# Four padded tiles: another start address for the weight halves and the activations of a two-layer trunk on one core

## The chip, the cores and the metric

One core of one Trainium2 chip runs the whole program. The metric is the time of one execution on the device, in microseconds (us). The kernel before was run three times, and its time is the median of the three.

## The reference, cut to what matters

The kernel computes a two-layer decoder trunk over 256 positions and 2048 channels, in float32. Each layer normalises its input, multiplies it with a wide input matrix, mixes along the sequence (layer 0: dilated attention and gated linear attention; layer 1: a diagonal state-space model, "S5", and gated linear recurrence heads), gates the result and multiplies it with an output matrix:

```python
def ab_layer(h, w_in, gla_w_gate, gla_b_gate, gla_norm_g, w_out):
    z = h @ w_in
    qa, ka, va, qb, kb, vb, g_low, gate = jnp.split(z, AB_SPLIT, axis=-1)
    ya = dilated_attention(...)
    ...
    y = jnp.concatenate([ya, yb], axis=-1) * jax.nn.silu(gate)
    return y @ w_out

def cd_layer(h, w_in, ...):
    z = h @ w_in
    u, qd, fd, idd, gate = jnp.split(z, CD_SPLIT, axis=-1)
    yc = s5_mixer(u, ...)
    ...
    y = jnp.concatenate([yc, yd], axis=-1) * jax.nn.silu(gate)
    return y @ w_out

# reference: h = h + layer(rmsnorm(h, norm_g[l]), ...) for both layers, then a final rmsnorm
```

Nearly all of the arithmetic is in `h @ w_in`, `y @ w_out` and one product with `s5_w_glu` inside the S5 mixer.

## The kernel before, in words

**Three products for one.** Every float32 operand of the large products is split into a high and a low part of the type float32r: the weights into `wh` (L168, ScalarE, a rounding copy) and `wl` (L169, VectorE, the rest), the activations into `xh` and `xl` (or `yh` and `yl`). A product is then wh·xh + wh·xl + wl·xh, so three matmuls stand for one.

**The stream of weights.** `load_split` fetches one group of weights (four k-tiles of 128 rows by 512 columns, 1 MB) into `raw`, splits it in two halves of two k-tiles each, and gives the halves to the matmuls. `raw`, `wh` and `wl` have three buffers each, in the pool `stream`.

**Two orientations.** A matmul on TensorE holds a stationary operand of 128 columns, loaded before (LDWEIGHTS), while the columns of a moving operand stream past it.
- `gemm_fm` (matmul at L181, output with features on the partitions): stationary is a 128-column piece of `wh` or `wl`, moving are the 256 columns of one k-tile of the activations. Twelve matmuls for each k-tile.
- `gemm_tm` (matmul at L200, output with time on the partitions): stationary is half a k-tile of the activations (128 columns), moving are 512 columns of `wh` or `wl`. Six matmuls for each k-tile.
- The last 512 output columns are done in two halves of 256 by `mms` (L755), with the activations stationary and 256 columns moving. In the first half the moving operand lies in the weight halves of the pool `stream`. In the second half the split weights are put into `xh` and `xl`, which are free by then, and move from there.

The profile names the moving operand first: `pg<-xh,wl` is a matmul with xh moving and wl stationary.

**Which activations.** `xh`/`xl` feed every product of an input matrix in both layers. `yh`/`yl` are allocated twice: in the pool `yp` for layer 0's output projection (372 to 463 us of the profile, `gemm_fm`), and again in the pool `yp2` for the S5 product `wg` (736 to 764 us, `gemm_fm`) and layer 1's output projection (811 us to the end, `gemm_tm` and `mms`).

**What sets the order.** The order of instructions on each engine is fixed when the program is built. TensorE runs the matmuls of the large products one after the other, and the small matmuls of attention, gated attention and S5 are put between them. Weight loads are issued by SyncE's queue.

**Where the tiles lie.** Pools are laid out one behind the other in each partition's SBUF, each tile rounded up to 32 bytes. The order is `const`, `stream`, `mix`, `small`, and then a stack: first `att`, with `prep` and later `yp` above it; after `att` and `yp` are closed, `gz`, with `s5` and later `yp2` above it. Sizes of `raw` (8192 bytes), `wh`, `wl` (4096 bytes each) and `xh`, `xl`, `yh`, `yl` (16384 bytes each, 1024 for a k-tile) are multiples of 512 bytes, as is the step of 128 columns (512 bytes) from one stationary piece to the next. So every buffer of one kind, and every piece of it that a matmul begins with, has the same start modulo 512 bytes. In the program before these starts are:

| tile (pool) | first byte in a partition | modulo 512 |
|---|---|---|
| xh, xl (const) | 33792, 50176 | 0 |
| ones (const) | 86816 | 288 |
| raw, wh, wl (stream) | 99936, 124512, 136800 | 96 |
| gq, gk, gv and others (mix) | 155232, 159328, 167520 | 96 |
| pT (att) | 191296 | 320 |
| yh, yl (yp) | 192832, 209216 | 320 |
| gz0, gz1 (gz) | 181056, 185152 | 320 |
| yh, yl (yp2) | 189248, 205632 | 320 |

Of the kernel before, what the change touches and what calls it, by code (L numbers as in the profile page):

```python
# [12 lines left out]
F32 = mybir.dt.float32  # L13
# [7 lines left out]
S = 256  # L21
# [36 lines left out]
def trunk(ctx: ExitStack, tc: tile.TileContext, I, out):  # L58
# [3 lines left out]
    const = ctx.enter_context(tc.tile_pool(name="const", bufs=1))  # L62
# [9 lines left out]
    def urgent():  # L72
        return tc.high_priority(offset=HI)
# [6 lines left out]
    oT = const.tile([128, KT, S], F32, name="oT")  # L80
    cst = const.tile([128, NCST], F32, name="cst")
    msk = const.tile([128, len(LV), 32], I32, name="msk")
    ones = const.tile([128, 128], F32, name="ones")
    sqa = const.tile([128, 4, S], F32, name="sqa")
    ident = cst[:, C_ID:C_ID + 128]

# [3 lines left out]
    def pm_tile(name="pm"):  # L90
        return pm.tile([128, 512], F32, name=name, tag="pm")
# [21 lines left out]
    def finish_norm(tag):  # L113
        V.tensor_add(sqa[:, 0:2], sqa[:, 0:2], sqa[:, 2:4])
        V.tensor_add(sqa[:, 0], sqa[:, 0], sqa[:, 1])
        ps = pm_tile()
        for t in range(2):
            T.matmul(ps[:, t:t + 1], sqa[:, 0, t * 128:(t + 1) * 128], ones[:, 0:1], start=True, stop=True)
        ms = small.tile([128, 2], F32, name="nms")
        V.tensor_scalar(ms, ps[:, 0:2], 1.0 / D, EPS, op0=OP.mult, op1=OP.add)  # L120
        rc = const.tile([128, 2], F32, name=tag + "c")
        rsqrt(rc, ms, 2, "nr")
        pb = pm_tile()
        for t in range(2):
            dg = small.tile([128, 128], F32, name="dg")
            V.tensor_scalar(dg, ident, rc[:, t:t + 1], None, op0=OP.mult)
            T.matmul(pb[:, t * 128:(t + 1) * 128], ones, dg, start=True, stop=True)
        rb = const.tile([128, S], F32, name=tag + "b")
        A.activation(rb, pb[:, 0:S], AF.Copy)
        return rc, rb  # L130
# [62 lines left out]
    def gemm_tm(src, groups, ah, al, mid=None, order=None):  # L193
        ps = pg.tile([128, 2, 512], F32, name="pg")
        last = groups * 4 - 1
        for i, kt, wh, wl in _iter(src, groups, mid, order):
            for n, (w, a) in enumerate(((wh, ah), (wh, al), (wl, ah))):
                for t in range(2):
                    ts_ = slice(t * 128, (t + 1) * 128)
                    state["mm"] = T.matmul(ps[:, t], a[:, kt, ts_], w, start=(i == 0 and n == 0),  # L200
                                           stop=(i == last and n == 2), skip_group_check=True)
        return ps
# [8 lines left out]
    def gla_tiles():  # L211
        return (mix.tile([128, 4, S], F32, name="gf"), mix.tile([128, 4, S], F32, name="gq"),
                mix.tile([128, 4, S], F32, name="gk"))

    att = ExitStack()
    ap_ = att.enter_context(tc.tile_pool(name="att", bufs=1))
# [23 lines left out]
    f, q, k = gla_tiles()  # L240
# [167 lines left out]
    def attention(h, q, k, v, vc):  # L408
        pr = ap_.tile([128, 2, S], F32, name="pr", bufs=1)
        mx = small.tile([128, 2], F32, name="amx")  # L410
        den = small.tile([128, 2], F32, name="aden")
        ps = pm_tile().rearrange("p (t j) -> p t j", t=2)
        for t in range(2):
            n = 128 * (t + 1)
            T.matmul(ps[:, t, 0:n], q[:, t * 128:(t + 1) * 128], k[:, 0:n], start=True, stop=True)  # L415
        for t in range(2):
            n = 128 * (t + 1)
            V.scalar_tensor_tensor(pr[:, t, 0:n], ps[:, t, 0:n], rsc[:, t:t + 1], bias[:, t, 0:n],
                                   op0=OP.mult, op1=OP.add)
            V.tensor_reduce(mx[:, t:t + 1], pr[:, t, 0:n], axis=mybir.AxisListType.X, op=OP.max)  # L420
        V.tensor_scalar(mx, mx, -1.0, None, op0=OP.mult)
        for t in range(2):
            n = 128 * (t + 1)
            A.activation(pr[:, t, 0:n], pr[:, t, 0:n], AF.Exp, bias=mx[:, t:t + 1], accum_out=den[:, t:t + 1])
        V.reciprocal(den, den)
        for t in range(2):
            n = 128 * (t + 1)
            V.tensor_scalar(pr[:, t, 0:n], pr[:, t, 0:n], den[:, t:t + 1], None, op0=OP.mult)
        pt = pm_tile()
        for n, (t, j) in enumerate(((0, 0), (1, 0), (1, 1))):  # L430
            T.transpose(pt[:, n * 128:(n + 1) * 128], pr[:, t, j * 128:(j + 1) * 128], ident)
        pT = ap_.tile([128, 384], F32, name="pT", bufs=1)
        A.activation(pT, pt[:, 0:384], AF.Copy)
        po = pm_tile()
        T.matmul(po[:, 0:256], v[:, 0, vc:vc + 128], pT[:, 0:256], start=True, stop=False)
        T.matmul(po[:, 128:256], v[:, 1, vc:vc + 128], pT[:, 256:384], start=False, stop=True)
        A.activation(oT[:, h], po[:, 0:256], AF.Copy)
# [14 lines left out]
    def heads(qk, h):  # L452
        for n in range(2):
            attention(h + n, qk[:, n], qk[:, 2 + n], v, (h + n) * 128)
# [34 lines left out]
    def gate_tm(src, rc, zs):  # L489
        ps = gemm_tm(src, 4, xh, xl)  # L490
        z = zs.rearrange("p a s -> p (a s)").rearrange("p (t d) -> p t d", t=2)
        with urgent():
            for t in range(2):
                A.activation(z[:, t], ps[:, t], AF.Silu, scale=rc[:, t:t + 1])
        return z
# [34 lines left out]
    with urgent():  # L530
        rc1, rb1 = finish_norm("r1")
# [3 lines left out]
    w1 = I["w1"]  # L535
    gz = ctx.enter_context(tc.tile_pool(name="gz", bufs=1))
# [124 lines left out]
    for half in range(2):  # L661
        f, q, k = gla_tiles()
# [8 lines left out]
        v = mix.tile([128, 2, 512], F32, name="gv")  # L671
        evac_tm(v, 0, gemm_tm(w1[4 + 3 * half], 4, xh, xl), rc1)
        gla(f, q, k, v, 128, 512 * half)
    zs2 = [gate_tm(w1[10 + n], rc1, gz.tile([128, 4, S], F32, name=f"gz{n}")) for n in range(2)]
    while fillq:
        hook()
    sp.close()
# [440 lines left out]
def build(arrays):  # L1118
    nc = bacc.Bacc("TRN2", target_bir_lowering=False, num_devices=1)
    I = {k: nc.dram_tensor("in_" + k + "_dram", v.shape, mybir.dt.from_np(v.dtype), kind="ExternalInput").ap()  # L1120
         for k, v in arrays.items()}
    out = nc.dram_tensor("out_0_dram", (2, 128, D), F32, kind="ExternalOutput").ap()
    with tile.TileContext(nc, schedule_with_timeline_sim=True) as tc:
        trunk(tc, I, out)
    if not nc.is_finalized():
        nc.finalize()
    return nc
# [8 lines left out]
```

## Time and profile before

| | us |
|---|---|
| median of 3 runs (912.89, 913.5, 915.94) | 913.5 |
| the profiled execution, its own time | 916.01 |
| its span, first to last instruction | 914.1 |
| TensorE busy in the span (98%) | 898.6 |
| VectorE busy (70%) | 637.1 |
| ScalarE busy (52%) | 472.1 |

The mean granted clock of TensorE is 0.993. The program moves 180.40 MB by DMA, 197 GB/s on average. Matmuls are pipelined: the busy time of one matmul overlaps that of the next, so the time that a stream of matmuls costs is read from the distance between the starts of successive ones, the pitch. The timeline merges consecutive matmuls with the same operands into a row (x4 is four of them) and gives the start of the first.

### The profile page before, as it was taken

What the parts mean: (1) busy time and instruction counts of PE and PEld (TensorE: products, weight loads), DVE (VectorE), ACT (ScalarE), POOL (GpSimd) and SP (SyncE); (2) the same over time, 40 slices, a digit from 0 to 9 for tenths busy, and PEclk for the clock granted to TensorE, in tenths of its full rate; (3) what the DMA queues carried; (4) which work ended last, traced back from release to release, by engine and by line L of the source; (5) the groups of instructions that cost most, each with busy time, mean ns of one, the idle gap of its engine ahead of it and who ended that gap; (6) DMA issues with size and microseconds to landing.
All of it is one profiled execution on the core that took longest, in us unless ns stands there. A gap on an engine that the chain in (4) does not pass through costs nothing.

```text
span 914.1 us, 18689 instructions
## 1 busy us (share of the span) xinstructions
PE 898.6 (98%) x7728; PEld 820.6 (90%) x7728; DVE 637.1 (70%) x1197; ACT 472.1 (52%) x715; POOL 54.4 (6%) x106
## 2 busy tenths in 40 slices
PE   9999899999999999999999999999999999999995
PEld 9987699978998899999999998799877799988885
DVE  7986874889859868755575585776987756555562
ACT  7554445665654765644443334445455465444451
POOL 0001100112101101000000001000100000000000
PEclk9999899999999999999999999999999999999998
DMA  9726643686746645555576665664643554555532
GB/s 319 304 102 204 225 177 142 195 271 219 261 186 218 219 179 184 191 185 185 185 276 197 242 235 192 222 207 142 223 169 116 200 204 157 187 177 182 185 138 92
DMA packets 40388, 180.40 MB, mean 197 GB/s; under 512 B 12720, under 2 KB 14256, under 8 KB 22768
## 3 DMA queue, kind: packets, MB, share of 16 engines
q1 hardware_dynamic: 29440, 154.99, 48.1%
q0 software_dynamic: 7984, 22.69, 7.5%
q10 hardware_dynamic: 2880, 1.54, 0.6%
q8 instruction: 60, 0.98, 0.4%
q14 instruction: 24, 0.20, 0.1%
HBM read 166.48 MB, written 12.71 MB: 196 GB/s over the span
## 4 chain that ended last, share of the span: by engine, by line
PE 94%; DMA 2%; DVE 1%; issue 1%; ACT 0%; POOL 0%; SPq 0%; POOLq 0%; DVEq 0%
PE pg L181 53%; PE pg L200 30%; PE pg L755 2%; PE pm L287 1%; PE pm L339 1%; DMA E<-ed 1%; PE pm L621 1%; PE pm L625 1%; PE pm L583 1%; PE pm L308 1%; PE pm L415 1%; DMA ed<-et 1%; PE pm L1024 1%; PE pm L504 0%; PE pm L711 0%
## 5 line engine op out<-in xcount | busy, mean ns | idle before, releaser
L168 ACT ACTIVATE wh<-raw 128x1024 fp32r<-128x1024 f32 (+2 forms) x276 | 287.7, 1046 | 350.9 <-PE pg L181 206.3
L169 DVE TENSOR_TENSOR wl<-raw,wh 128x1024 fp32r<-128x1024 f32 (+2 forms) x276 | 332.6, 1207 | 179.4 <-ACT wh L168 174.5
L181 PE MATMUL pg<-xh,wl 128*128 128x256 f32 x1024 | 167.3, 283 | 0.0
L181 PE MATMUL pg<-xh,wh 128*128 128x256 f32 x1024 | 166.2, 283 | 0.5 <-ACT wh L168 0.5
L181 PE MATMUL pg<-xl,wh 128*128 128x256 f32 x1024 | 165.8, 282 | 0.0
L181 PEld LDWEIGHTS pg<-xh,wh 128*128 128x128 f32 x1024 | 140.1, 189 | 1.9 <-ACT wh L168 1.2
L181 PEld LDWEIGHTS pg<-xh,wl 128*128 128x128 f32 x1024 | 140.7, 189 | 1.0 <-DVE wl L169 0.3
L181 PEld LDWEIGHTS pg<-xl,wh 128*128 128x128 f32 x1024 | 140.6, 189 | 0.6 <-issue 0.3
L200 PE MATMUL pg<-wl,xh 128*128 128x512 f32 x320 | 103.2, 403 | 3.0 <-DVE wl L169 3.0
L200 PE MATMUL pg<-wh,xl 128*128 128x512 f32 x320 | 102.8, 401 | 0.0
L200 PE MATMUL pg<-wh,xh 128*128 128x512 f32 x320 | 102.5, 401 | 0.0
L200 PEld LDWEIGHTS pg<-wl,xh 128*128 128x128 f32 x320 | 59.8, 190 | 18.2 <-DVE wl L169 4.0
L200 PEld LDWEIGHTS pg<-wh,xl 128*128 128x128 f32 x320 | 60.4, 190 | 14.5
L200 PEld LDWEIGHTS pg<-wh,xh 128*128 128x128 f32 x320 | 60.1, 190 | 14.0
L181 PE MATMUL pg<-yh,wh 128*128 128x256 f32 x320 | 51.3, 281 | 0.0
L181 PE MATMUL pg<-yh,wl 128*128 128x256 f32 x320 | 50.8, 281 | 0.0
L181 PE MATMUL pg<-yl,wh 128*128 128x256 f32 x320 | 50.8, 281 | 0.0
L181 PEld LDWEIGHTS pg<-yh,wh 128*128 128x128 f32 x320 | 43.6, 188 | 0.0
L181 PEld LDWEIGHTS pg<-yl,wh 128*128 128x128 f32 x320 | 43.5, 188 | 0.0
L181 PEld LDWEIGHTS pg<-yh,wl 128*128 128x128 f32 x320 | 43.4, 188 | 0.0
L964 POOL DMA_DIRECT2D tabs<-pc x44 | 23.8, 547 | 167.0 <-DVE x L974 42.6
L200 PE MATMUL pg<-wh,yh 128*128 128x512 f32 x96 | 30.4, 398 | 0.0
(350 smaller groups left out, 1008.9 us busy)
## 6 DMA issues: line engine op xcount, KB each, us to landing
raw<-in_w_dram SPq DMA_DIRECT2D x100, 1024.0 KB, 5.0
raw<-in_wo_dram SPq DMA_DIRECT2D x28, 1024.0 KB, 4.8
tb<-tabs POOLq DMA_DIRECT2D x8, 768.0 KB, 6.3
tabs<-pc POOLq DMA_DIRECT2D x20, 256.0 KB, 5.5
raw<-in_wg_dram SPq DMA_DIRECT2D x4, 1024.0 KB, 4.8
raw<-in_wo1l_dram SPq DMA_DIRECT2D x4, 1024.0 KB, 4.8
raw<-in_w_dram SPq DMA_DIRECT2D x6, 512.0 KB, 7.6
tabs<-pc POOLq DMA_DIRECT2D x24, 128.0 KB, 4.3
```

The lines of the kernel that those rows point to most:

```text
L168: state["wh"] = A.activation(w, r, AF.Copy)
L169: V.tensor_sub(l, r, w)
L181: state["mm"] = T.matmul(ps[:, c], w[:, cs], a[:, kt], start=(i == 0 and n == 0 and c % 2 == 0), stop=(i == last and n == 2), skip_group_c ...
L200: state["mm"] = T.matmul(ps[:, t], a[:, kt, ts_], w, start=(i == 0 and n == 0), stop=(i == last and n == 2), skip_group_check=True)
L287: T.matmul(ps[32 * b:32 * b + 32, t, hd], k[:, hd, r], Q[:, hd, r], start=True, stop=True)
L308: T.matmul(ps[j0:j0 + h, hd, j0 + h:j0 + 2 * h], k[:, hd, b:b + h], Qp[:, hd, b + h:b + 2 * h], start=True, stop=True)
L339: T.matmul(ps[:, (hd - h0) * dv:(hd - h0 + 1) * dv], AT[:, hd, t + j], v[:, j, hd * dv:(hd + 1) * dv], start=(j == 0), stop=(j == t))
L415: T.matmul(ps[:, t, 0:n], q[:, t * 128:(t + 1) * 128], k[:, 0:n], start=True, stop=True)
L583: T.matmul(pv[g * 64:g * 64 + 64, w, pr], t["W"][w][us, 4 * h + pr], X[us, g, 4 * h + pr], start=True, stop=True)
L621: T.matmul(py[g * 64:g * 64 + 64, pr], w[:, pr], X[:, g, pr], start=(pr == 0), stop=False, skip_group_check=True)
L755: T.matmul(ps[:, t, 0:256], a_[:, kt, ts_], w_, start=(kt == 0 and n == 0), stop=(kt == KT - 1 and n == 2), skip_group_check=True)
L964: nc.gpsimd.dma_start(tabs[qt, dst, n], t[src].rearrange("p a b -> p (a b)"))
```

## The change

Four tile declarations get columns behind their data that nothing reads or writes. No instruction is added, removed or given another shape; only start addresses change.

```diff
-    ones = const.tile([128, 128], F32, name="ones")
+    ones = const.tile([128, 128 + 56], F32, name="ones")[:, 0:128]
...
-        pT = ap_.tile([128, 384], F32, name="pT", bufs=1)
+        pT = ap_.tile([128, 384 + 8], F32, name="pT", bufs=1)[:, 0:384]
...
-    zs2 = [gate_tm(w1[10 + n], rc1, gz.tile([128, 4, S], F32, name=f"gz{n}")) for n in range(2)]
+    zs2 = [gate_tm(w1[10 + n], rc1, gz.tile([128, 4 * S + 24 * n], F32, name=f"gz{n}")[:, 0:4 * S]
+                   .rearrange("p (a s) -> p a s", a=4)) for n in range(2)]
```

The 56 columns behind `ones` (224 bytes) move everything laid out after it by 224 bytes. The 8 columns behind `pT` (32 bytes) move `prep` and `yp` by 32 more. Behind `gz0` stand 24·0 = 0 columns, behind `gz1` 24 (96 bytes), which move `s5` and `yp2` by 96 more. Modulo 512 bytes this gives:

| tile | before | after |
|---|---|---|
| xh, xl | 0 | 0 |
| raw, wh, wl, and the pool mix | 96 | 320 |
| yh, yl of layer 0 (yp) | 320 | 320 + 256 = 64 |
| yh, yl of layer 1 (yp2) | 320 | 320 + 320 = 128 |

## The prediction

> **What bounds the kernel now.** I read the page first: engine shares, the chain that ended last, the costliest groups. Then the waits of TensorE, and then the timeline, where the change has to show.
>
> ```profile
> PE 898.6 (98%) x7728; PEld 820.6 (90%) x7728; DVE 637.1 (70%) x1197; ACT 472.1 (52%) x715; POOL 54.4 (6%) x106
> PE 94%; DMA 2%; DVE 1%; issue 1%; ACT 0%; POOL 0%; SPq 0%; POOLq 0%; DVEq 0%
> L168 ACT ACTIVATE wh<-raw 128x1024 fp32r<-128x1024 f32 (+2 forms) x276 | 287.7, 1046 | 350.9 <-PE pg L181 206.3
> L181 PE MATMUL pg<-xh,wl 128*128 128x256 f32 x1024 | 167.3, 283 | 0.0
> L200 PE MATMUL pg<-wl,xh 128*128 128x512 f32 x320 | 103.2, 403 | 3.0 <-DVE wl L169 3.0
> L181 PE MATMUL pg<-yh,wh 128*128 128x256 f32 x320 | 51.3, 281 | 0.0
> L200 PE MATMUL pg<-wh,yh 128*128 128x512 f32 x96 | 30.4, 398 | 0.0
> L755 PE MATMUL pg<-wh,yh 128*128 128x256 f32 x32 | 9.0, 282 | 0.0
> PE pg L200 <- DVE wl L169: 3.0, 2, 2.8
> PE pg L181 <- ACT wh L168: 0.5, 1, 0.5
> ```
>
> TensorE is busy for 98% of the span and holds 94% of the chain. It waits for data 3.0 + 0.5 us, while ScalarE's rounding copy stands idle 206.3 us behind the L181 matmuls because its buffers are still in use. So the time is the number of matmuls times their pitch. The groups give the numbers, each with three products: feature-major with xh/xl 3 x 1024 = 3072, with yh/yl 3 x 320 = 960, time-major 3 x (320 + 96) = 1248, and at L755 32 a group, 96 in each half. A mean of 283 ns is no price, since matmuls overlap; the pitch is. The timeline gives it from the first and the last row of an undisturbed stretch:
>
> ```profile
> 488.01 0.63 PE L181 MATMUL pg<-xh,wh 128*128 128x256 f32 x4
> ...
> 507.72 0.51 PE L181 MATMUL pg<-xh,wh 128*128 128x256 f32 x3
> ...
> 777.80 0.63 PE L181 MATMUL pg<-xl,wh 128*128 128x256 f32 x4
> ...
> 797.73 0.52 PE L181 MATMUL pg<-xl,wh 128*128 128x256 f32 x3
> ...
> 375.48 0.63 PE L181 MATMUL pg<-yl,wh 128*128 128x256 f32 x4
> ...
> 399.61 0.64 PE L181 MATMUL pg<-yl,wh 128*128 128x256 f32 x4
> ...
> 174.03 0.63 PE L200 MATMUL pg<-wh,xh 128*128 128x512 f32 x2
> ...
> 193.62 0.63 PE L200 MATMUL pg<-wh,xh 128*128 128x512 f32 x2
> ...
> 811.88 0.63 PE L200 MATMUL pg<-wl,yh 128*128 128x512 f32 x2
> ...
> 832.88 0.40 PE L200 MATMUL pg<-wl,yh 128*128 128x512 f32 x1
> ...
> 881.11 0.28 PE L755 MATMUL pg<-wh,yh 128*128 128x256 f32 x1
> ...
> 891.61 0.28 PE L755 MATMUL pg<-wh,yh 128*128 128x256 f32 x1
> ...
> 893.33 0.28 PE L755 MATMUL pg<-xh,yh 128*128 128x256 f32 x1
> ...
> 896.73 0.28 PE L755 MATMUL pg<-xh,yh 128*128 128x256 f32 x1
> ```
>
> The pairs are 168, 168, 204, 84, 90, 90 and 30 matmuls apart (whole k-tiles of 12 or 6, or whole rounds of three products). With the starts modulo 512 bytes from the table above, written stationary/moving:
>
> - feature-major, xh: 96/0, two rates: 19.71 us / 168 = 117.3 ns and 19.93 / 168 = 118.6
> - feature-major, yh: 96/320: 24.13 / 204 = 118.3
> - time-major, 512 columns, xh: 0/96: 19.59 / 84 = 233.2; yh: 320/96: 21.00 / 90 = 233.3
> - L755, first half, 256 columns: 320/96: 10.50 / 90 = 116.7
> - L755, second half, 256 columns: 320/0: 3.40 / 30 = **113.3**
>
> The last two are the key. They have the same shape, the same kind of operands and the same stationary tile; only the moving operand starts at 0 instead of 96, and the pitch falls by 3.3 ns. The first line has the same moving start 0 and the same width as the last, but stationary 96 instead of 320, and is 4.0 to 5.3 ns slower. So, as far as these rows go, the pitch depends on start addresses, and 96 is a bad start on either side. I read 96 as bad because it isn't a multiple of 64, as 0, 64, 128 and 320 are; the rows fit that, but show no other odd start, so it is a guess.
>
> **The change part by part.** No instruction, DMA, wait or buffer is added or removed, and the order in each queue stays. What moves is the residue pairs:
>
> 1. Feature-major with xh/xl, 3072 matmuls, 96/0 becomes **320/0**: the pair of the 113.3 row. Their clean pitches run from 117.3 to 118.6; I take 118.0, near the middle. 3072 x (118.0 - 113.3) = 14.4 us. Bounds: gain 14.4; loss, if the new pair falls to the worst pitch at 256 columns that the trace has, 120 ns (rows below), 3072 x 2.0 = 6.1 us.
> 2. Feature-major with yh/yl, 960, 96/320 becomes 320/64 (768 in the output projection) and 320/128 (192 in `wg`). No row has a moving start of 64 or 128. Bounds: 113.3 and 120, so -4.8 to +1.6 us. I take -4.8, because 320 as stationary and starts that are multiples of 64 are what the 113.3 row has.
> 3. Time-major, 1248, 0/96 and 320/96 become 0/320 and 320/128. The stationary start made no difference (233.2 against 233.3), and 233.3 is twice the 116.7 of 256 columns at the same moving 96. If moving away from 96 saves per column what it saves at L755, 512 columns go to 2 x 113.3 = 226.7: -6.7 ns x 1248 = -8.3 us. If what is left at 113.3 is partly a price per matmul, more falls away. Other bound: 2 x 120, +8.3 us. I take -8.3.
> 4. L755: first half 320/96 becomes 128/320, 96 x -3.3 ns = -0.3 us. Second half 320/0 becomes 128/0: it has the best row now, so nothing to -0.3 and up to 96 x 6.7 = +0.6 us; I take nothing.
> 5. The casts at L168 and L169, the loads and the small matmuls: source and destination of the casts move together, by 224 bytes. I cost them at nothing: ScalarE waits on TensorE here, and VectorE has the cover of the next rows. If each of the 276 casts on VectorE were a tenth longer (0.12 of 1.2 us), the busiest stages would come to its limit.
>
> ```profile
> L169 DVE TENSOR_TENSOR wl<-raw,wh 128x1024 fp32r<-128x1024 f32 (+2 forms) x276 | 332.6, 1207 | 179.4 <-ACT wh L168 174.5
> 0.00:30.00 30.00, 28.46 (x202) 27.72 (x203) 24.77 (x91) 22.59 (x37) 1.76 (x7) 1.00 0.94 342
> 172.00:220.00 48.00, 48.00 (x238) 38.51 (x238) 40.38 (x89) 28.80 (x55) 7.63 (x14) 1.00 0.76 247
> 76.72 5.07 DMA ed<-et
> 82.07 10.14 DMA E<-ed
> 94.80 1.15 DVE wl L169
> ```
>
> The columns of the two windows are length, then busy time of PE, PEld, DVE, ACT, POOL, then clock, DMA share, GB/s. Two places don't give their gain back in full. In the first 30 us the weights come at 342 GB/s with the DMA engines busy for 0.94, so TensorE can't run ahead of the loads. From 76.72 to 95.95 us the chain runs through S5's two transfers (5.07 and 10.14 us) and VectorE. These 49 us are 5% of the span: 5% of 27.8 is 1.5 us. VectorE, busy for 40.38 of 48.00 us, would be at 40.38 / 46.6 = 87% after a stage 3% shorter: no bound, but it may delay a cast once or twice, 0.5 us as an estimate from the 3.0 us that it costs now. I take off 2 us.
>
> Sum: 14.4 + 4.8 + 8.3 + 0.3 - 2.0 = 25.8 us against the profiled execution's 916.0: **890**. That execution is 2.5 us above the median. The two rates of 96/0 can make such a difference (3072 x 1.3 ns = 4.0 us between all slow and all fast). The other pairs show one rate, so I expect the new kernel at one level and don't take the 2.5 us off again.
>
> [...]
>
> **The rivals.**
>
> *Only the pair that the trace has gets faster.* The new pairs at 64, 128 and 0/320 keep their pitches and step 1 alone stands: 916.0 - 14.4 + 1 = 903; with step 2 or step 3 beside it 894 to 898. For it: a rule from two good starts is thin. Against: 96/0 and 96/320 both lie at 117 to 118.6, so nothing shows 320 as moving start to be worse than 0.
>
> *The change doesn't do what it says in the feature-major stream.* The 113.3 row differs from L181 in more than addresses: L181 sends successive matmuls to four parts of two PSUM banks and moves the same columns four times, L755 stays in one part and changes the moving columns. If that makes the 4 to 5 ns, steps 1 and 2 bring nothing, and only time-major gains: 916.0 - 8.3 = 908, or, without it, 914, the old time.
>
> *Slower: the new pairs clash.* If the two reads of one matmul disturb each other by their distance, not by a bad start, a new distance can be worse. A row for it is a small product with stationary `glhl` (320 and steps of 128 bytes on) and xh or xl moving at 0:
>
> ```profile
> 49.39 0.28 PE L372 MATMUL pm<-xh,glhl 128*32 128x256 f32 x1
> ...
> 52.87 0.28 PE L373 MATMUL pm<-xl,glhl 128*16 128x256 f32 x1
> ```
>
> 3.48 us / 29 = 120 ns, slower than any other stream of 256 columns, though every start is a multiple of 64. Its stationary operand is only 32 or 16 columns wide, so I don't take it for the rule. If feature-major fell to 120 ns: 6.1 + 1.6 = +7.7 us, 924. It decides from the point where the feature-major pitch passes 118.0 with time-major unchanged.
>
> **How the numbers follow.** All steps as costed: 0.48, 884 to 895 by its own bounds. Only part of them (893 to 904): 0.22. Nothing in feature-major: 0.16 (0.07 near 908, 0.09 unchanged). Slower, 924: 0.14. A measurement here can tell 0.3% from no change, 2.7 us: 910.8 to 916.2. That gives faster 0.48 + 0.22 + 0.07 = 0.77, same 0.09, slower 0.14. The range must reach to the unchanged time to leave out no more than 2 in 10: 882 to 914; 882 allows for time-major some 6 ns better than 226.7, less the losses.
>
> **What would show it.** In the profile after: feature-major pitch with xh at 113.3 in the clean stretches (step 1), with yh in the output projection at 113.3 (step 2), time-major at 226.7 (step 3), each at one rate. TensorE still near 98% busy, its waits for `wl` and `wh` under 6 us in sum (step 5). L755's second half unchanged (step 4). The prediction is wrong if the feature-major pitch with 320/0 isn't that of the L755 row, if a moving start of 64, 128 or 320 costs what 96 costs, or if VectorE's casts become the chain.

## The result, and the profile after

The kernel after takes 898.8 us (median of four, 898.14 to 899.84) against 913.5 us: ratio 0.9835, 95% interval 0.9815 to 0.9855. The profiled execution took 898.85 us, its span is 897.0 us. The prediction was 890 in a range of 882 to 914: the time lies inside the range, 9 us over the sum.

From the page of the kernel after, the engine shares and the chain by engine, then two waits of TensorE, as before:

```profile
PE 880.9 (98%) x7728; PEld 806.7 (90%) x7728; DVE 636.2 (71%) x1197; ACT 472.5 (53%) x715; POOL 54.4 (6%) x106
PE 88%; DVE 4%; DMA 2%; ACT 2%; issue 2%; SPq 0%; POOL 0%; POOLq 0%; DVEq 0%
PE pg L181 <- ACT wh L168: 2.3, 3, 1.1
PE pg L200 <- DVE wl L169: 0.5, 2, 0.3
```

TensorE's busy time fell by 17.7 us, the span by 17.1; VectorE and ScalarE are as they were. TensorE's part of the chain fell from 94% to 88%, and the rest runs through casts, loads and issue, but its waits stay small (2.3 + 0.5 us for `wh` and `wl`). So it is still mainly the pitch. The timeline of TensorE in the kernel after, first and last row of a stretch for each pair (L755 is now L756):

```profile
485.37 0.62 PE L181 MATMUL pg<-xh,wh 128*128 128x256 f32 x4
...
504.41 0.62 PE L181 MATMUL pg<-xh,wh 128*128 128x256 f32 x4
...
31.55 0.64 PE L181 MATMUL pg<-xh,wh 128*128 128x256 f32 x4
...
38.62 0.64 PE L181 MATMUL pg<-xh,wh 128*128 128x256 f32 x4
...
435.59 0.64 PE L181 MATMUL pg<-yh,wh 128*128 128x256 f32 x4
...
451.43 0.64 PE L181 MATMUL pg<-yh,wh 128*128 128x256 f32 x4
...
735.72 0.63 PE L181 MATMUL pg<-yh,wh 128*128 128x256 f32 x4
...
746.55 0.63 PE L181 MATMUL pg<-yh,wl 128*128 128x256 f32 x4
...
165.45 0.62 PE L200 MATMUL pg<-wh,xl 128*128 128x512 f32 x2
...
184.68 0.62 PE L200 MATMUL pg<-wh,xl 128*128 128x512 f32 x2
...
816.94 0.63 PE L200 MATMUL pg<-wh,yl 128*128 128x512 f32 x2
...
837.47 0.63 PE L200 MATMUL pg<-wh,yh 128*128 128x512 f32 x2
...
863.13 0.28 PE L756 MATMUL pg<-wh,yl 128*128 128x256 f32 x1
...
873.38 0.28 PE L756 MATMUL pg<-wh,yl 128*128 128x256 f32 x1
```

The counts between are 168, 60, 132, 92, 84, 88 and 87 matmuls. As stationary/moving modulo 512 bytes:

| matmuls | pair before | ns before | pair after | ns after | foretold |
|---|---|---|---|---|---|
| feature-major xh, 3072 | 96/0 | 117.3 or 118.6 | 320/0 | 113.3, in places 117.8; mean 114.0 | 113.3 |
| feature-major yh, layer 0, 768 | 96/320 | 118.3 | 320/64 | 120.0 | 113.3 |
| feature-major yh, `wg`, 192 | 96/320 | 118.4 | 320/128 | 117.7 | 113.3 |
| time-major xh, 960 | 0/96 | 233.3 | 0/320 | 228.9 to 229.2 | 226.7 |
| time-major yh, 288 | 320/96 | 233.3 | 128/320 | 233.3 | 226.7 |
| L756 first half, 96 | 320/96 | 116.7 | 128/320 | 117.8 | 113.3 |

### The profile page after: what moved, and what is told of

Its sections match the earlier page's. It is cut to its first block, busy times and chain, and to the rows that moved or that the text cites. A ratio compares the mean times of both kernels' runs of the same rounds, so it can differ in the third digit from the quotient of the medians.

```text
span 897.0 us, 18689 instructions
## 1 busy us (share of the span) xinstructions
PE 880.9 (98%) x7728; PEld 806.7 (90%) x7728; DVE 636.2 (71%) x1197; ACT 472.5 (53%) x715; POOL 54.4 (6%) x106
## 4 chain that ended last, share of the span: by engine, by line
PE 88%; DVE 4%; DMA 2%; ACT 2%; issue 2%; SPq 0%; POOL 0%; POOLq 0%; DVEq 0%
PE pg L181 51%; PE pg L200 26%; PE pg L756 2%; PE pm L287 1%; PE pm L339 1%; PE pm L621 1%; DMA E<-ed 1%; PE pm L625 1%; DVE wl L169 1%; DMA raw<-in_w_dram 1%; PE pm L583 1%; PE pm L308 1%; PE pm L415 1%; PE pm L1025 1%; ACT wh L168 1%
## 5 line engine op out<-in xcount | busy, mean ns | idle before, releaser
L181 PE MATMUL pg<-xh,wh 128*128 128x256 f32 x1024 | 161.8, 279 | 2.3 <-ACT wh L168 2.3
L181 PE MATMUL pg<-xh,wl 128*128 128x256 f32 x1024 | 163.1, 280 | 0.1
L181 PE MATMUL pg<-xl,wh 128*128 128x256 f32 x1024 | 161.1, 278 | 0.0
L181 PEld LDWEIGHTS pg<-xh,wh 128*128 128x128 f32 x1024 | 136.6, 188 | 4.0 <-ACT wh L168 3.4
L181 PEld LDWEIGHTS pg<-xh,wl 128*128 128x128 f32 x1024 | 136.9, 188 | 1.3 <-DVE wl L169 0.5
L181 PEld LDWEIGHTS pg<-xl,wh 128*128 128x128 f32 x1024 | 136.7, 188 | 0.6 <-issue 0.3
L200 PE MATMUL pg<-wl,xh 128*128 128x512 f32 x320 | 101.0, 396 | 0.7 <-DVE wl L169 0.5
L200 PE MATMUL pg<-wh,xl 128*128 128x512 f32 x320 | 100.7, 394 | 0.0
L200 PE MATMUL pg<-wh,xh 128*128 128x512 f32 x320 | 100.3, 394 | 0.0
L200 PEld LDWEIGHTS pg<-wl,xh 128*128 128x128 f32 x320 | 59.1, 188 | 14.2 <-DVE wl L169 1.6
L200 PEld LDWEIGHTS pg<-wh,xl 128*128 128x128 f32 x320 | 59.8, 188 | 12.9
L200 PEld LDWEIGHTS pg<-wh,xh 128*128 128x128 f32 x320 | 59.3, 188 | 12.8
L181 PE MATMUL pg<-yh,wh 128*128 128x256 f32 x320 | 51.8, 283 | 0.0
L181 PE MATMUL pg<-yh,wl 128*128 128x256 f32 x320 | 51.3, 282 | 0.0
L181 PE MATMUL pg<-yl,wh 128*128 128x256 f32 x320 | 51.3, 282 | 0.0
L181 PEld LDWEIGHTS pg<-yh,wh 128*128 128x128 f32 x320 | 44.1, 191 | 0.0
L181 PEld LDWEIGHTS pg<-yl,wh 128*128 128x128 f32 x320 | 44.0, 191 | 0.0
L181 PEld LDWEIGHTS pg<-yh,wl 128*128 128x128 f32 x320 | 44.0, 191 | 0.0
L200 PE MATMUL pg<-wh,yh 128*128 128x512 f32 x96 | 30.4, 397 | 0.0
```

The costliest lines, as they stand in the source:

```text
L181: state["mm"] = T.matmul(ps[:, c], w[:, cs], a[:, kt], start=(i == 0 and n == 0 and c % 2 == 0), stop=(i == last and n == 2), skip_group_c ...
```

## The experiments

Theory 1, the prediction's: each start counts by itself, multiples of 64 are good. It was in trouble at once, since 320/64 and 128/320 are no better than before. Theory 2: the distance from the stationary to the moving start decides. Theory 3: the trunk's other work sets the pitch.

**1. and 2. All pairs, alone.** A program without the trunk: 16 stationary by 16 moving starts, 32 bytes apart, 48 matmuls of 256 columns a pair (bench256), or 28 of 512 (bench512).

```python
p = ps.tile([128, 512], F32, name="s" + chr(97 + i) + "m" + chr(97 + j), tag="p")
for r in range(REPS):
    c, k = r % PIECES, (r // PIECES) % 2
    T.matmul(p[:, 0:N], sta[:, 8*i + 128*c:8*i + 128*c + 128], mov[:, 8*j + N*k:8*j + N*k + N], ...)
```

> This program leaves out the trunk: it runs 256 streams of 48 matmuls of 256 columns, one stream for each pair of a stationary start (letter after s: a = 0, b = 32, ... p = 480 modulo 512 bytes) and a moving start (letter after m), the four stationary pieces in turn as in the feature-major product, and nothing else beside them. Theory 1, own start: what counts is whether each of the two starts is a multiple of 64. Then the 64 pairs with two such starts run at 113.3 ns and the others at 116.7 to 118.7. Theory 2, distance: the pitch depends on moving minus stationary start modulo 512 alone, one value on each diagonal: 113.3 at 192, 120 at 256, about 118 at 224 and 320, 117.3 or 118.7 at 416, 116.7 at 288. Theory 3, neither: 320/0, 320/64 and 320/128 don't come out at the 113.3, 120.0 and 117.8 of the kernel after, so that the trunk's other work sets the pitch; then the table is flat or has another order.

> This program leaves out the trunk: as the one with 256 columns, but 28 matmuls of 512 columns a stream with two stationary pieces in turn, as in the time-major product. Own start: all pairs with a moving start that is a multiple of 64 run alike, faster than 233.3 ns. Distance: one value on each diagonal, 229.1 ns where moving minus stationary is 320, 233.3 at 96, 192 and 288. If the trunk's other work sets the pitch, the 0/320 stream doesn't come out near 229.1.

From the timelines, stationary start 32 (`sb`), moving 32, 64, 96 and 288, 320, 352, first 256 columns, then 512. Columns are start and length in us:

```profile
107.82 5.92 PE L82 MATMUL sbmb<-mov,sta 128*128 128x256 f32 x48
113.57 5.82 PE L82 MATMUL sbmc<-mov,sta 128*128 128x256 f32 x48
119.23 5.82 PE L82 MATMUL sbmd<-mov,sta 128*128 128x256 f32 x48
...
153.36 5.92 PE L82 MATMUL sbmj<-mov,sta 128*128 128x256 f32 x48
159.11 5.82 PE L82 MATMUL sbmk<-mov,sta 128*128 128x256 f32 x48
164.77 5.82 PE L82 MATMUL sbml<-mov,sta 128*128 128x256 f32 x48
```

```profile
120.52 6.53 PE L82 MATMUL sbmb<-mov,sta 128*128 128x512 f32 x28
126.89 6.70 PE L82 MATMUL sbmc<-mov,sta 128*128 128x512 f32 x28
...
172.53 6.53 PE L82 MATMUL sbmj<-mov,sta 128*128 128x512 f32 x28
178.90 6.70 PE L82 MATMUL sbmk<-mov,sta 128*128 128x512 f32 x28
```

A stream and the one 256 bytes further have the same length, and at one distance all 16 stationary starts agree, the first stream of all (48 matmuls in 8.34 us, 174 ns each) and the two distances with two pitches aside. Means of the later part of each stream, good to some 0.3 ns:

| moving minus stationary, modulo 256 bytes | 0 | 32 | 64 | 96 | 128 | 160 | 192 | 224 |
|---|---|---|---|---|---|---|---|---|
| 256 columns, ns | 120.0 | 117.8 | 117.8 | 120.1 | 118.5 | 118.6 or 117.3 | 117.8 or 113.3 | 118.3 |
| 512 columns, ns | 226.7 | 233.3 | 229.1 | 233.2 | 233.1 | 234.3 | 233.3 | 233.3 |

Theory 2 is right among starts that are multiples of 32, with a period of 256, not 512. Every pitch of the trunk, before and after, stands in this table but L755's first half before (116.7 at distance 32, where the table has 117.8; the pair 0/32 stands at 116.7 in the programs of experiments 6 and 10 too, so this distance has a second pitch). Theories 1 and 3 fall. For 256 columns, 192 can have 113.3, and then the same two tiles in the time-major product have 256 - 192 = 64: 229.1. The change puts the weights and xh just there. It puts layer 0's yh at distance 0, with 96 the slowest.

**3. Everything 32 bytes further.** `xv` gets 12 columns more, which with the rounding to 32 bytes moves every tile behind it by 32; the rest is as in the kernel after.

> The kernel after with 48 bytes more behind xv, so that every tile behind it moves by 32 bytes: xh at 32, weight halves at 352, yh at 96 and 160. All distances stay. Distance theory: the pitches of the kernel after, 113.3, 120.0, 117.8, 229.1, 233.3 ns, and 899 us. Own start theory: no start is a multiple of 64 any more, the pitches go back to those of before, 117 to 119 and 233.3, and the time to about 913 us.

898.7 us, ratio 0.9838 (0.9816 to 0.9861), mean pitches 114.0, 120.0, 117.8, 229.2, 233.3. Starts don't count by themselves at this grain; distances do.

**4. The pad behind ones alone.** pT and gz1 as in the kernel before.

> The columns behind ones alone; those behind pT and gz1 taken away, so that yh and yl start at 32 in both layers and the weight halves at 320 as in the kernel after. Distance theory: layer 0's output projection 0 to 224, 120.0 to 118.3, -1.3 us; the S5 product 64 to 224, 117.8 to 118.3, +0.1; time-major of layer 1 192 to 32, 233.3 both. So 897.6 us: the other two pads of the change cost about 1 us. Own start theory: yh at 32 is a bad start, 3 us or more slower than the kernel after, 902.

Its timeline in layer 0's output projection, 336 matmuls:

```profile
379.98 0.64 PE L181 MATMUL pg<-yl,wh 128*128 128x256 f32 x4
...
419.74 0.52 PE L181 MATMUL pg<-yl,wh 128*128 128x256 f32 x3
```

39.76 us / 336 = 118.3 ns, as the distance 224 has it, and 899.7 us (898.0 to 901.3; ratio 0.9844, 0.9818 to 0.9869). The median is 2 us over what was expected. The profiled execution, at 898.0 us the fastest of the four, is near it, with feature-major with xh at a mean of 114.4, against 114.0 in the kernel after, more of it at the slower of its two pitches; what the slower three did isn't shown. The whole measured gain of the change comes with the pad behind `ones`; the other two (behind `pT` and `gz1`, as `gz0` gets no column) can't be told from nothing in the time, and by pitch cost 768 x 1.7 = 1.3 us less 0.1.

**5. yh where the table wants it.** Distance 192 for feature-major and 64 for time-major in both layers. Against the kernel after:

```diff
-        pT = ap_.tile([128, 384 + 8], ...)[:, 0:384]
+        pT = ap_.tile([128, 384 + 8 + 48], ...)[:, 0:384]
-    ... gz.tile([128, 4 * S + 24 * n], ...)
+    ... gz.tile([128, 4 * S + 56 * n], ...)
```

> The kernel after with yh and yl put at 256 instead of 64 (layer 0) and 128 (layer 1), by wider columns behind pT and gz1. Distance theory (moving minus stationary, modulo 256): layer 0's output projection goes from 0 to 192, 120.0 to 113.3 ns on 768 matmuls, -5.1 us; the S5 product from 64 to 192, 117.8 to 113.3 on 192, -0.9; layer 1's time-major products from 192 to 64, 233.3 to 229.1 on 288, -1.2; L756's second half from 128 to 0, 118.7 to 120, +0.1. Sum -7.1, so 892 against 899 us; 895 to 896 if the slower of the two pitches at 192 (117.8) holds throughout. Own start theory (multiples of 64 are good): no change, 899, since 64, 128 and 256 are alike.

```profile
390.23 0.62 PE L181 MATMUL pg<-yl,wh 128*128 128x256 f32 x4
...
428.31 0.62 PE L181 MATMUL pg<-yl,wh 128*128 128x256 f32 x4
```

38.08 us / 336 = 113.3 ns, `wg` 114.0, time-major 229.0 in layer 1: all as the table has it. Time 894.4 us (893.2 to 897.6), ratio 0.9788 (0.9761 to 0.9815). In the profiled execution, 895.6 us, feature-major with xh ran at a mean of 114.8. That is 3072 x 0.8 = 2.5 us over the kernel after, of the 3.6 us by which this execution lies over the 892.

**6. and 7. Steps of 4 bytes, and the phase of entry.** Programs without the trunk.

> This program leaves out the trunk. Stationary start fixed at 0. Streams fXX: 256 columns, moving start 4 bytes further each time, 0 to 252. Streams tXX: the same with 512 columns. Streams qXX: 256 columns at distance 192, each behind one matmul of 4, 8, ... 256 columns, so that it is entered at another phase. The distance between the moving and the stationary start decides, as the two tables showed (period 256 bytes, every 32). If the reads go in blocks of 32 bytes or more, the steps of 4 bytes between two table points give nothing better than their neighbours; if finer, a distance better than 113.3 or 226.7 ns can turn up. At distance 192 two pitches were seen, 113.3 (6 of 32 streams) and 117.8 (26). If the phase of entry chooses between them, the q streams split into these two; if something else does (the start itself), all are alike.

> This program leaves out the trunk. 32 streams of 48 matmuls of 256 columns at each of the distances 16 (b), 112 (c), 144 (d), 192 (e), 0 (g), 160 (h) bytes, and 24 of 512 columns at 0 (u) and 64 (v), each entered behind one matmul of another width. If the pitch of 113.3 ns is one of two at every distance where it was seen, b, c and d split as e does (at 192 it was 24 of 64 streams, the others 117.8). If it is the only one at some distance, all 32 streams of that letter stand at 113.3, and feature-major products put at that distance would keep it. At 0 one pitch is expected, 120.0, at 160 two, 117.3 and 118.7; with 512 columns one each, 226.7 and 229.1.

Steps of 4 bytes: 256 columns give 113.3 at the distances 16, 112, 144 and 192, other steps up to 123.3; with 512 columns nothing beats 226.7, and steps of 4 bytes off a multiple of 16 reach 240.0. The q streams split, 26 at 113.3 and 38 at 117.8 (the 24 named in the next expectation is a miscount). In entry_phase all 32 streams at 112 (`c`) stand at 113.3, those at 192 (`e`) split 13 to 19, those at 16 are mostly at 116.7 and at 144 at 118.7. Two of each from the timeline, behind leads of 24 and 44 columns:

```profile
204.04 5.72 PE L81 MATMUL cac<-mov,sta 128*128 128x256 f32 x48
...
220.80 5.72 PE L81 MATMUL caf<-mov,sta 128*128 128x256 f32 x48
...
569.09 5.90 PE L81 MATMUL eac<-mov,sta 128*128 128x256 f32 x48
...
586.38 5.71 PE L81 MATMUL eaf<-mov,sta 128*128 128x256 f32 x48
```

So at 192 the entry chooses one of two pitches, 113.3 or 117.8 ns, which then stay. The trunk shows both as well, a stretch between two pauses being at one of them. The same 376 matmuls, at 320/0 in both kernels, in the kernel after and then in y_at_256:

```profile
749.24 0.62 PE L181 MATMUL pg<-xl,wh 128*128 128x256 f32 x4
...
791.85 0.62 PE L181 MATMUL pg<-xh,wl 128*128 128x256 f32 x4
...
745.40 0.63 PE L181 MATMUL pg<-xl,wh 128*128 128x256 f32 x4
...
789.68 0.64 PE L181 MATMUL pg<-xh,wl 128*128 128x256 f32 x4
```

42.61 us / 376 = 113.3 ns and 44.28 / 376 = 117.8. That each pause for a small matmul is a new entry fits this. How much of the scatter between executions it makes isn't shown.

**8. Two starts for the weights.** Wider weight halves, used from 144 for feature-major (distance 112 to xh at 0) and from 0 for time-major; r1b shares r0b's place, the order of instructions stays.

```diff
-            wh = stream.tile([128, 2, 512], F32R, name="wh", bufs=3)
-            wl = stream.tile([128, 2, 512], F32R, name="wl", bufs=3)
+            wh, wl = [stream.tile([128, 1024 + 64], F32R, name=n, bufs=3)[:, off:off + 1024]
+                      .rearrange("p (k c) -> p k c", k=2) for n in ("wh", "wl")]
...
```

> The weight halves get 64 columns more, and feature-major products use them from 144 modulo 256, time-major ones from 0; xh, yh and yl start at 0 modulo 256, L756's first half moves from 112. Distances: feature-major 112, time-major 0, L756 first half 112, second half 0. r1b shares r0b's place to make room; order of instructions as in the kernel after. Distance theory: feature-major 113.3 ns throughout with no share at 117.8 (against 114.8 on average in y_at_256, -4.3 us on 3072), time-major 226.7 (-2.4 ns on 1248, -3.0), L756 first half 113.3 (-0.4). So about 887 us, 7 under y_at_256, and executions closer together, since no distance with two pitches is left in the large products. If the trunk's waits take the gain back, the pitches come out so and the time stays above 891.

```profile
390.17 0.64 PE L181 MATMUL pg<-yh,wh 128*128 128x256 f32 x4
...
429.05 0.64 PE L181 MATMUL pg<-yh,wh 128*128 128x256 f32 x4
```

A miss: 38.88 us / 324 = 120.0 ns, and 910.4 us (ratio 0.9951, 0.9932 to 0.9970). Time-major came out (226.9 in layer 1), and so did L756's first half at 0/112 (mean 113.8). Only 144/0 didn't, though its distance is 112 too.

**9. All distances 0.**

> The kernel after with other pads: weight halves, xh, yh and yl all at 0 modulo 256, so all distances are 0. Distance theory: feature-major 120.0 ns, the worst of the table (4032 matmuls, about +7.7 us against the kernel before), time-major 226.7, the best (1248, -8.4), L756 120.0 (+0.9 us). The two cancel: 913 to 914 us, as before, with quite other pitches. Own start theory (multiples of 64 are good): all starts are good, 890 us as in the prediction.

912.3 us, ratio 0.9974 (0.9959 to 0.9988), with feature-major at 119.9 to 120.0 and time-major at 226.9 to 227.6. The time is nearly that of before with every pitch changed: the worst distance of one product is the best of the other.

**10. Where 144/0 went.** Without the trunk, starts by 16 bytes.

> This program leaves out the trunk. Starts in steps of 16 bytes: stationary 0 or 16, moving 0 to 240, four streams a pair entered behind matmuls of 32, 68, 100 and 140 columns, 256 columns (f) and 512 (t); and the pairs 144/0, 112/112, 112/0 and 48/176. In two_starts the pair 144/0 ran at 120.0 ns, though its distance 112 gave 113.3 in every one of 32 streams where the stationary start was 0. If that was the trunk's doing, 144/0 runs at 113.3 here. If the distance decides only among starts that are multiples of 32, and the 16 bytes within a block of 32 count on each side by themselves, 144/0 runs at 120.0 here too, 0/112 at 113.3, and the row of stationary start 16 isn't the row of 0 moved along by 16.

Four pairs from its timeline, 40 matmuls of 256 columns each: 0/112, 0/192, 16/208, 144/0, all behind a lead of 68 columns, and then 20 of 512 columns, 0/64 and 16/80:

```profile
422.75 4.82 PE L80 MATMUL fahb<-mov,sta 128*128 128x256 f32 x40
...
470.69 4.96 PE L80 MATMUL famb<-mov,sta 128*128 128x256 f32 x40
...
633.66 4.83 PE L80 MATMUL fbnb<-mov,sta 128*128 128x256 f32 x40
...
662.30 5.03 PE L80 MATMUL fcab<-mov,sta 128*128 128x256 f32 x40
...
398.80 4.83 PE L80 MATMUL taeb<-mov,sta 128*128 128x512 f32 x20
...
561.76 4.78 PE L80 MATMUL tbfb<-mov,sta 128*128 128x512 f32 x20
```

144/0 ends at 120.0 in three of four streams without the trunk as well, 0/112 at 113.3 in four. So theory 2 has a limit: the distance decides only among pairs whose starts lie at the same places in a block of 32 bytes. 144/0 (places 16 and 0) goes with 16/128, at 120.0 in all four streams, and not with 0/112 (places 0 and 16). With both starts 16 into a block, 16/208 (distance 192) is at 113.3 in all four streams, where 0/192 has two pitches, and 16/80 (distance 64) takes 226.7 for 512 columns instead of 229.1.

**11. The pairs of y_at_256, 16 bytes into the block.** One start for the weights again.

```diff
+    def at(pool, name, off, pad):
+        return pool.tile([128, KT * S + pad], F32R, name=name)[:, off:off + KT * S].rearrange("p (k s) -> p k s", k=KT)
-    xh = const.tile([128, KT, S], F32R, name="xh")
+    xh = at(const, "xh", 4, 64)
...
```

> The pairs of y_at_256, all moved by 16 bytes inside a block of 32: xh, xl, yh, yl start at 16 modulo 256 and the weight halves at 80 for both orientations (208 for L756's first half). Distances as in y_at_256: feature-major 192, time-major 64. Room is made as in two_starts. In the table by 16 bytes, 16/208 stood at 113.3 ns in all four streams, where 0/192 had two pitches, and 16/80 with 512 columns at 226.7, where 0/64 has 229.1. If the table holds in the trunk: feature-major 113.3 on 4032 matmuls (y_at_256 had 114.8 on 3072 of them, -4.3 us), time-major 226.7 on 1248 (-2.9), L756 first half 113.3 (-0.4), second half 118.3 (-0.2). So 887 us, 7 to 8 under y_at_256, with less scatter. If only the distance counted, the time would be that of y_at_256, 894.

Feature-major with yh in layer 0 (348 matmuls), then time-major with xh (78):

```profile
389.88 0.61 PE L184 MATMUL pg<-yh,wh 128*128 128x256 f32 x4
...
429.32 0.61 PE L184 MATMUL pg<-yh,wh 128*128 128x256 f32 x4
...
165.02 0.61 PE L203 MATMUL pg<-wh,xh 128*128 128x512 f32 x2
...
182.70 0.61 PE L203 MATMUL pg<-wh,xh 128*128 128x512 f32 x2
```

39.44 us / 348 = 113.3, 17.68 / 78 = 226.7, feature-major with xh 113.7 on average. 887.4 us (886.1 to 889.9), ratio 0.9712 (0.9691 to 0.9732): 11 us under the kernel after and the fastest here. The smaller scatter that was expected didn't come: the five executions span 3.8 us, those of y_at_256 4.4.

## Why the prediction was right, and where it was wrong

The measured 898.8 us is inside the range, but outside the 884 to 895 of "all steps as costed". It is the case that the prediction had called "only part of them" (893 to 904, chance 0.22): step 1 and half of step 3. That it lies inside the range in spite of steps 2 and 3 is luck: the range reached to the unchanged time, and the rule behind these steps was wrong.

*What bounds the kernel* held: the pitch of the large products is the time, and no step brought a new wait of size.

*Step 1* (feature-major with xh) held, by the row it was taken from: 113.3 at 320/0. The reason given, that 96 is a bad start in itself, did not: what changed is the distance, from 160 to 192. It brought 3072 x (118.0 - 114.0) = 12.3 us of the 14.4. The missing 2 us are the second pitch of distance 192, which the short stretch of L755 didn't show; the prediction had "one level" here, and it isn't one.

*Step 2* (yh) is the step that failed. It took 64 and 128 as good starts; the distances are 0 and 64, and layer 0's went to 120.0, the end that the prediction had put as its upper bound. In place of a gain of 4.8 us it cost 768 x 1.7 - 192 x 0.6 = 1.2 us.

*Step 3* (time-major) had the right sign for xh and was mis-sized: -4.2 ns a matmul, not -6.7, 960 x 4.2 = 4.0 us; with yh nothing. 226.7 exists, but at distance 0 (experiment 9) or 16 bytes into the block (11), not at 64.

*Step 4* had the wrong sign: L756 lost 96 x 1.1 ns in its first half and 96 x 5.0 in its second, 0.6 us.

*The losses*, 2 us, didn't come: beside the pitches another 17.1 - (12.3 - 1.2 + 4.0 - 0.6) = 2.6 us went away. Most of that isn't pitch but clock. In the profiled execution of the kernel before, TensorE had half its clock for some 6.8 us, from the end of its 2.8 us wait for `wl` after S5's transfers on. First two windows, the clock third from last, then two pieces of the chain:

```profile
83.00:114.00 31.00, 28.18 (x217) 21.45 (x216) 21.60 (x35) 14.12 (x20) 3.27 (x6) 0.89 0.69 212
95.40:102.20 6.80, 6.21 (x15) 4.92 (x16) 6.79 (x9) 1.06 (x1) 1.15 (x2) 0.50 0.70 232
...
95.99 8.67 PE pg L200 x24
104.85 5.79 PE pg L200 x24
```

24 matmuls took 8.67 us there and the next 24 took 5.79, so 2.9 us were lost. The profiled execution of the kernel after has no such stretch: its clock is 1.00 from 5 to 880 us. Waits at L200 for `wl` fell by 2.5 us and at L181 for `wh` rose by 1.8, and two new ones (L287 and L431) took 0.8 + 0.4. With the pitches' 14.5 us this makes 14.5 + 2.9 + 2.5 - 1.8 - 1.2 = 16.9 of the 17.1. The prediction had put the 2.5 us by which this execution lay over the median down to the two rates of 96/0; the clock is the likelier reason. The ten executions of the kernel before with a mean clock of 0.996 in the experiments took 911.4 to 913.3 us, the six with 0.993 914.6 to 919.9. So a part of the measured gain, up to some 3 us, is not the pitch. Whether the wait brings the low clock, no run here shows.

The guess behind steps 2 and 3, multiples of 64, rested on 96 being the only bad start in sight. One row spoke against it: the 120 ns of the product with `glhl`, whose starts are all multiples of 64, was put aside. It doesn't follow from distance either, as by its starts it alternates between 192 and 64, where the table has 117.8 and at best 113.3; its stationary operand is narrower. The rival "slower: the new pairs clash" named what decides, distance, and it came true for 768 of the matmuls (120.0 ns); that two reads disturb each other, as it supposes, no run shows. The rival by feature-major's own structure fell: L181 reaches 113.3 itself, and bench256 finds its pitches by address alone, with one part of PSUM written by each stream.

With one moving start, the stationary start alone moves the pitch. Feature-major with xh at 0 ran at 117.3 to 118.6 ns with the weights at 96, at 113.3 or 117.8 with them at 320, and at 119.9 to 120.0 with them at 0 modulo 256 (experiment 9). No stream of 256 columns here was faster than 113.3.

## What to carry to other kernels

Where matmuls stand back to back, read the pitch from the starts in the timeline, not the mean duration, and compare it between stages with the same shape: 113.3 against 118 ns in one trace is a hint that addresses matter. Then measure the pairs of start addresses by themselves in one small program before padding, and choose the start of each tile by the distance to the operand it meets, in each orientation in which it is used. Measure the starts with the places within 32 bytes that the tiles will have, and check the table in the kernel, since a rule that fits five rows may be the wrong one. And look at the granted clock in both traces (here it was 0.50 for some 6.8 us in the kernel before) before all of a gain is put down to the pitch. The tables here are for float32r operands; no other type was measured so.

## What the runs showed that was not expected

- The pitch of float32r matmuls, among starts that are multiples of 32, goes by the distance between the operands' starts and repeats with 256 bytes: 113.3 to 120.1 ns at 256 columns, 226.7 to 234.3 at 512.
- The same pair of starts can have two stable pitches (at distance 192, 113.3 in 13 of 32 streams and 117.8 in 19); which of the two is settled on entry.
- 16 bytes on both sides make one of two pitches the only one seen (16/208, four streams) and 512 columns 2.4 ns faster (16/80). Why is open: no run here shows it, and the starts between multiples of 16 were tried with stationary start 0 alone.
